# One layer of a gated three-branch decoder step: x loaded ahead of the modulation weights and kept transposed, the start ordered by hand, query statistics a step earlier

## The chip, the core and the metric

The kernel runs on one core of one Trainium2 chip. The time is the device time of one execution in microseconds (us); three runs of the kernel before have the median 1188.63. The engines are called PE (TensorE, the matrix multiplier), DVE (VectorE), ACT (ScalarE), POOL (GpSimd) and SP (SyncE, which here only issues DMAs). Each takes its instructions in the order in which they stand in its own queue.

## What is computed

Eight sample sequences of 8 tokens and one prompt of 1024 tokens, 1088 tokens of 1024 channels in all, pass one layer:

```python
mod = silu(c) @ ada_w + ada_b                      # c: one row for the prompt, eight for the samples
shift, scale, gate = split(mod, 3)
h = rmsnorm(x, norm_g) * (1.0 + scale) + shift
z = h @ w_in + b_in                                # some 8,500 + 3 * 1024 columns, split among:
ya = chunk_gmlp(a_u, a_v, ...) * silu(a_g)         # A: spatial gating in chunks of 128
yb = swa_branch(b_q, b_k, b_v, ...) * silu(b_g)    # B: sliding-window attention, 8 heads of 64, 2 of K and V
yc = mlstm_branch(c_qk, c_v, ...) * silu(c_g)      # C: matrix memory, short convolution on q and k
gates = sigmoid(m_g)                               # three per channel
merged = gates[0] * (ya @ w_branch_a) + gates[1] * (yb @ w_branch_b) + gates[2] * (yc @ w_branch_c)
x_out = x + gate * (merged @ w_out)
```

In branch B, q and k are normalised by head (an rmsnorm over 64 values) before the logits. The states of the branches are outputs as well.

## The kernel before

All is in float32. Matrix products are made of split operands: a high part, rounded to the multiplier's own format (float32r), and the rest, so that one product takes three matmuls (high by high, high by low, low by high). A split is a copy into the high part, mostly on ACT, and a subtraction on DVE. The names hh and hl are the high and low parts of h for each of its eight groups k of 128 channels, transposed to channels by tokens; hl without a number is also the name of a split slab of weights.

**The start** (the pool named start) makes h and the product with the first slab of w_in. x comes in nine tiles of 128 tokens (xt; the last, xts, holds the 64 sample tokens). A tile is squared and summed on ACT (L322), POOL makes the reciprocal root (L162 and L163) and DVE scales the tile in place (L325). The modulation comes in four blocks j, of two channel groups each: a block's weights are four loads of 512 KB (adaraw). PE multiplies them with silu(c) in 32 small matmuls (named adaraw,sT), ACT copies the result (msb, L356), PE turns it with eight matmuls (sel,msb), and DVE makes modA and modB of it (L366, L368). For a channel group k and a third ci of the tokens (384, 384 and 320 of them) three transposes on PE bring x into a PSUM tile (pk), ACT applies modA and modB (hf, L382), and DVE makes hh (L388) and hl (L389). Then PE multiplies with the two halves i of slab 0: 48 steps of three matmuls, 96 matmuls of 384 columns and 48 of 320. The weights of slab 0 are copied on ACT and subtracted on POOL (L277, L278).

The order of the start before is given by two strings. LOADS lists SP's loads: `x0 r x1 x2 a0 w0 a1 w1 x3 x4 x5 a2 x6 x7 x8 a3 s`, where a0 to a3 are the modulation's blocks, w0 and w1 the halves of slab 0, r and s small rows. STEPS is the order of the program, in which N is a group of three tiles of x, M a block, and 010 means groups 0 to 1 of third 0, each at once followed by its matmuls. A scheduler then orders each engine's instructions.

**Branch B** runs as a pipeline of 16 steps in two query groups g, eight token tiles n each, with other branches' products as filler; one step takes between 7 and 8 us. PE's order in it is that of the program. For each step the tile's queries are transposed on PE (L89), copied on ACT into the high part of QT (L1039) and subtracted on DVE (L1040). The statistics of the queries are made for three tiles at once (q_stats): squares and sums on DVE (L1011, L1012), a root on POOL. For the tiles 6 to 8 they are issued at step n = 6. Tile 8 holds the sample tokens: its queries are scaled ahead of the transposes, by two multiplications of 64x128 (qraw<-qraw,r, L1020), and split into QTs at step 7. K is transposed and split ahead of the pipeline into KT (L986, L987).

**The merge** has three rounds n of four pairs p. In a round PE makes the gates of a pair from h, and projects y with the branch weights (proj, which DVE evacuates at L1686); one pair takes some 33 us. Ahead of rounds 1 and 2, y_load reads the next branch's y from DRAM in eight pieces into a buffer of two halves (stage) and splits each piece into yh (ACT, L1649) and yl. The multiplication of branch B's result with its gate (gate_b) uses the same two halves for its two operands: it loads both, multiplies on DVE (L1757) and stores the product. Before, the multiplies of gate_b run as soon as their loads land.

Of the kernel before, what the change touches and what calls it, by code (L numbers as in the profile page):

```python
# [31 lines left out]
NORM1 = (0, 1, 2)  # L32
# [6 lines left out]
def trunk_kernel(ctx: ExitStack, tc: tile.TileContext, I, O):  # L39
# [197 lines left out]
    with tc.tile_pool(name="start", bufs=1, side="right", reuse_waits="tile") as st:  # L237
# [31 lines left out]

        hl0 = wp.tile([128, 2, 2112], F32R, tag="hl", bufs=2, name="hl")  # L270
        cur[0] = 1

        def slab0_load(i):
            raw = hp.tile([128, 1024], F32, tag=f"h{'hl'[i]}3", name="raw0")
            nc.sync.dma_start(raw.rearrange("p (k c) -> p k c", k=8), specs[0][i])
            o = slice(1024 * i, 1024 * i + 1024)
            S.copy(hl0[:, 0, o], raw)  # L277
            G.tensor_tensor(hl0[:, 1, o], raw, hl0[:, 0, o].bitcast(F32), ALU.subtract)  # L278
# [40 lines left out]
        def norm1(n):  # L319
            tn = TILES[n][1]  # L320
            junk = st.tile([128, 1024], F32, name="junk")
            S.activation(junk[:tn], xt[n][:tn], AF.Square, accum_out=ss[:tn, n:n + 1])  # L322
            y = rst[:, n:n + 1]
            rsqrt(y, ss[:, n:n + 1], 1024)
            V.tensor_scalar(xt[n][:tn], xt[n][:tn], y[:tn], None, ALU.mult)  # L325

        def norm(g):
            if g in NORM1:
                for n in range(3 * g, 3 * g + 3):
                    norm1(n)  # L330
                return
            sl = slice(3 * g, 3 * g + 3)
            for n in range(3 * g, 3 * g + 3):
                tn = TILES[n][1]
                junk = st.tile([128, 1024], F32, name="junk")
                S.activation(junk[:tn], xt[n][:tn], AF.Square, accum_out=ss[:tn, n:n + 1])
            rsqrt(rst[:, sl], ss[:, sl], 1024)
            for n in range(3 * g, 3 * g + 3):
                tn = TILES[n][1]
                V.tensor_scalar(xt[n][:tn], xt[n][:tn], rst[:tn, n:n + 1], None, ALU.mult)  # L340
# [7 lines left out]
        def mod(j):  # L348
# [7 lines left out]
            last["s"] = S.copy(msb, pm)  # L356
            pc = pk()
            if j == 0:
                tr(pc[:, 128:160], Ra)
                V.tensor_copy(cols[:, CADA:CADA + 32], pc[:, 128:160])  # L360
                V.tensor_scalar(cols[:, CADA + 8:CADA + 16], cols[:, CADA + 8:CADA + 16], 1.0, None, ALU.add)
            for q in range(4):
                mm(pc[:, 16 * q:16 * q + 9], msb[:, 128 * q:128 * q + 128], sel, True, True)
            for d in range(2):
                k = 2 * j + d
                last["m"] = V.tensor_scalar(modA[:, k], pc[:, 16 * d:16 * d + 9], cols[:, CADA + 8 + k:CADA + 9 + k],  # L366
                                cols[:, CNG + k:CNG + k + 1], ALU.add, ALU.mult)
                V.tensor_scalar(modB[:, k], pc[:, 32 + 16 * d:32 + 16 * d + 9], cols[:, CADA + k:CADA + k + 1],  # L368
                                None, ALU.add)

        def hprep(k, ci):
# [5 lines left out]
            px = pk()  # L377
            for i in range(3):
                t0, tn = TILES[3 * ci + i]
                tr(px[:, 128 * i:128 * i + tn], xt[3 * ci + i][:tn, 128 * k:128 * k + 128])  # L380
# [9 lines left out]
            if m < n:  # L390
                S.copy(hh[k][:, NT:1152], hlo[k][:, 1024:NT].bitcast(F32))
# [4 lines left out]
        def part(k, ci, i):  # L396
            c0, n = CH[ci]
            if (ci, i) not in acc:
                acc[ci, i] = pg() if 2 * ci + i < 3 else pu_()
# [8 lines left out]
        for step in STEPS.split():  # L408
            if step == "P":
                with tc.issue_after(last["m"].ins), tc.issue_after(last["s"].ins):  # L410
                    load_pieces(1, [None] * 3 + [st.tile([128, 528], F32, name="raw1")])
            elif step == "S":
                ps = pk()
                tr(ps[:, 0:68], R1)
                V.tensor_copy(cols[:, 0:CADA], ps[:, 0:CADA])
                V.tensor_copy(cols[:, CCB:100], ps[:, CADA:68])
            elif step[0] == "N":
                norm(int(step[1]))
            elif step[0] == "M":
                mod(int(step[1]))  # L420
            else:
                ci = int(step[2])
                for k in range(int(step[0]), int(step[1]) + 1):
                    hprep(k, ci)
                    for i in range(2 if ci < 2 else 1):
                        part(k, ci, i)
        for k in range(8):
            part(k, 2, 1)
# [419 lines left out]
    with tc.tile_pool(name="bph", bufs=1, side="right", reuse_waits="tile") as b1:  # L848
# [125 lines left out]
        def k_transpose(n):  # L974
# [9 lines left out]
            for g in range(2):  # L984
                o, i = slice(128 * n + 128, 128 * n + 256), slice(128 * g, 128 * g + 128)
                S.copy(KT[g][0][:, o], ps[:, i])  # L986
                V.tensor_tensor(KT[g][1][:, o], ps[:, i], KT[g][0][:, o].bitcast(F32), ALU.subtract)  # L987
# [18 lines left out]
        def q_stats(g, n0):  # L1006
# [7 lines left out]
            r3 = bt([128, 3, 4], "r3", bufs=2)  # L1014
            rsqrt(r3.rearrange("p n h -> p (n h)"), rf, 64)
            r3s[g] = r3
# [8 lines left out]
        def q_transpose(g, n):  # L1025
# [5 lines left out]
            for r in range(2):  # L1031
# [7 lines left out]
                S.copy(hi, src)  # L1039
                newq[0] = V.tensor_tensor(lo, src, hi.bitcast(F32), ALU.subtract).ins  # L1040
# [5 lines left out]
        class Prompt:  # L1046
# [224 lines left out]
        def a_norm():  # L1271
            vr = bt([128, 9], "vr", tag="rr", bufs=2)
            vq = bt([128, 9], "vq", tag="r3", bufs=2)
# [81 lines left out]
        for i in range(len(steps) + 6):  # L1355
            w = FILL[0] if i < 18 else FILL[1]
            for d, ph, share in PLAN:
                if 0 <= i - d < len(steps):
                    if ph == "q" and i < 16:
                        filler(0, ("q", i // 8, min(8, i % 8 // 3 * 3 + 2)))  # L1360
# [304 lines left out]
    def proj(n, f, Tt):  # L1665
# [5 lines left out]
        def run(t):  # L1671
            if n == 2 and f % 4 == 3:
                m_tiles(f)
            for h in range(2):
                for j in range(2):
# [9 lines left out]
                    with tc.high_priority():  # L1685
                        V.scalar_tensor_tensor(x, x, 1.0, ps, ALU.add, ALU.mult)  # L1686
# [9 lines left out]
    gst = {}  # L1696
# [53 lines left out]
    def gate_b(f, b):  # L1750
# [6 lines left out]
        V.tensor_tensor(x, x, y, ALU.mult)  # L1757
# [117 lines left out]
```

## Time and profile before

| | |
|---|---|
| median of three runs | 1188.63 us (1188.22 to 1191.99) |
| the profiled execution | 1185.67 us, span 1184.0 us |
| mean granted clock of PE | 0.997 |
| PE's waits over 1 us behind the first 60 us | 3.7, 1.2, 1.2 and 1.0 us |
| bytes moved | 129.73 MB, 110 GB/s over the span |

The profile is of one execution. A row of a timeline gives the start in us, the length, the engine, the line of the code, the instruction, what it writes and reads, the partitions by elements, and how many such stand in a row (x); in brackets how long the engine was idle before it, and what ended that. PE's instructions overlap, so that the time of one is read from the distance between two starts. A row of waits gives the engine, what it waited to do, the releaser, and us in total, times, and the longest. A row of windows gives the stretch, its length, the busy time of each engine, PE's granted clock (1.00 is full speed), the busy share of the DMA engines and the GB/s.

### The profile page before, as it was taken

The numbers are of one execution on the slowest core, as the hardware profiler recorded it, in microseconds if no ns is written. First come the engines' busy times: TensorE is split into PE (matmuls) and PEld (weight loads), VectorE is DVE, ScalarE is ACT, GpSimd is POOL, SyncE is SP. The second block draws the span as 40 slices with busy tenths as digits, with TensorE's granted clock in tenths as the row PEclk, the third lists the DMA queues.
The fourth block names the chain that finished last, engine by engine and source line by source line (L and its number), as shares of the span: only waits on it lengthen the run. The fifth ranks groups of instructions, "written<-read, shape, count | busy, mean of one in ns | idle before, by whom it ended". The sixth has DMA issues, their size and how long they took to land.

```text
span 1184.0 us, 23111 instructions
## 1 busy us (share of the span) xinstructions
PE 1154.9 (98%) x8924; PEld 1108.1 (94%) x8924; DVE 777.7 (66%) x1846; ACT 489.0 (41%) x1225; POOL 81.3 (7%) x111
## 2 busy tenths in 40 slices
PE   5899999999999999989999999999999999999998
PEld 2699999999999998978998999999999999999998
DVE  3577877655468587876598973655766676668433
ACT  4543455434343368877353441423322343235100
POOL 2100011102024001110000000000000000000000
PEclk9999999999999999989999999999999999999999
DMA  9821222323222110123235256424543354465422
GB/s 309 256 73 37 76 84 64 103 64 100 90 79 75 51 54 15 55 63 96 63 95 154 55 166 190 135 76 120 162 115 109 108 166 116 130 208 177 130 90 73
DMA packets 150773, 129.73 MB, mean 110 GB/s; under 512 B 13614, under 2 KB 140214, under 8 KB 150649
## 3 DMA queue, kind: packets, MB, share of 16 engines
q1 hardware_dynamic: 142984, 118.96, 34.1%
q0 software_dynamic: 2240, 7.08, 1.7%
q10 hardware_dynamic: 5440, 2.23, 0.7%
q8 instruction: 70, 1.15, 0.4%
q14 instruction: 39, 0.31, 0.1%
HBM read 99.39 MB, written 29.82 MB: 109 GB/s over the span
## 4 chain that ended last, share of the span: by engine, by line
PE 85%; DMA 5%; DVE 4%; ACT 2%; issue 1%; SPq 1%; POOL 0%; ACTq 0%; DVEq 0%
PE pg L85 47%; PE pk L85 22%; PE pu L85 13%; PE pk L89 2%; DMA stage<-dy 2%; DMA raw<-in_w_in_dram 1%; DMA dy<-stage 1%; SPq L251 1%; ACT Sm L1080 1%; DVE hl L125 1%; PE pu L89 1%; DVE Sm L1072 0%; DVE nm L1075 0%; DVE QT L1040 0%; DVE rr L1012 0%
## 5 line engine op out<-in xcount | busy, mean ns | idle before, releaser
L85 PE MATMUL pg<-hl,hl 128*128 128x256 f32 (+3 forms) x904 | 278.5, 308 | 0.8 <-DVE hl L389 0.8
L85 PE MATMUL pg<-hh,hl 128*128 128x384 f32 (+1 forms) x912 | 238.3, 335 | 3.4 <-DVE hh L388 2.3
L85 PE MATMUL pg<-hl,hh 128*128 128x256 f32 (+1 forms) x1008 | 178.0, 283 | 0.0
L85 PEld LDWEIGHTS pg<-hl,hl 128*128 128x128 f32 x904 | 170.9, 189 | 3.9 <-DVE hl L389 1.7
L85 PEld LDWEIGHTS pg<-hh,hl 128*128 128x128 f32 x912 | 161.9, 189 | 7.8 <-DVE hh L388 3.9
L85 PEld LDWEIGHTS pg<-hl,hh 128*128 128x128 f32 x1008 | 150.8, 189 | 0.3
L1408 ACT CAST prod<-raw 128x512 fp32r<-128x512 f32 x76 | 46.8, 620 | 125.0 <-PE pk L85 51.7
L85 PE MATMUL pg<-hh,prod 128*128 128x288 f32 (+1 forms) x400 | 83.9, 289 | 0.2 <-DVE prod L1409 0.2
L85 PE MATMUL pk<-hh,prod 128*128 128x256 f32 (+1 forms) x384 | 78.1, 285 | 0.0
L1572 ACT ACTIVATE tt<-tt,bh 128x288 f32<-128x288 f32 x96 | 49.8, 522 | 47.5 <-DVE tt L1517 16.2
L1409 DVE TENSOR_TENSOR prod<-raw,prod 128x512 fp32r<-128x512 f32 x76 | 51.8, 686 | 24.2 <-ACT prod L1408 24.0
L85 PEld LDWEIGHTS pg<-hh,prod 128*128 128x128 f32 x400 | 65.8, 188 | 1.1 <-issue 0.4
L85 PEld LDWEIGHTS pk<-hh,prod 128*128 128x128 f32 x384 | 62.6, 188 | 0.8 <-DVE tt L1526 0.4
L1408 ACT CAST prod<-comb 128x512 fp32r<-128x512 f32 x60 | 36.9, 615 | 62.1 <-PE pk L85 25.5
L85 PE MATMUL pg<-yh,prod 128*128 128x288 f32 (+1 forms) x288 | 60.9, 290 | 0.0
L85 PE MATMUL pk<-yh,prod 128*128 128x256 f32 (+1 forms) x288 | 58.7, 285 | 0.0
L85 PE MATMUL pg<-hl,prod 128*128 128x288 f32 (+1 forms) x200 | 57.7, 289 | 0.0
L85 PE MATMUL pu<-hh,prod 128*128 128x288 f32 (+1 forms) x272 | 56.3, 288 | 0.0
L85 PE MATMUL pk<-tc,prod 128*128 128x256 f32 (+1 forms) x408 | 56.2, 287 | 0.0
L85 PE MATMUL pg<-tc,prod 128*128 128x288 f32 (+1 forms) x396 | 55.7, 290 | 0.0
L85 PE MATMUL pk<-hl,prod 128*128 128x256 f32 (+1 forms) x192 | 54.6, 284 | 0.0
L85 PEld LDWEIGHTS pk<-tc,prod 128*128 128x128 f32 x408 | 52.6, 188 | 1.3 <-issue 0.8
(532 smaller groups left out, 2635.8 us busy)
## 6 DMA issues: line engine op xcount, KB each, us to landing
raw<-in_w_in_dram SPq DMA_DIRECT2D x124, 256.0 KB
adaraw<-in_ada_w_dram SPq DMA_DIRECT2D x16, 512.0 KB
stage<-dy SPq DMA_DIRECT2D x24, 272.0 KB
dmg<-tt SPq DMA_DIRECT2D x44, 144.0 KB
dmg<-tt SPq DMA_DIRECT2D x44, 128.0 KB
mprev<-dmg SPq DMA_DIRECT2D x32, 144.0 KB
xt<-in_x_prompt_dram SPq DMA_DIRECT2D x8, 512.0 KB
graw<-in_ada_w_dram SPq DMA_DIRECT2D x16, 256.0 KB
```

Of the source, the lines that this page charges most:

```text
L85: T.matmul(out, lhsT=lhsT, rhs=rhs, start=start, stop=stop)
L89: T.transpose(out, in_, ident[:k, :k])
L125: V.tensor_tensor(hl[:, 1, off:off + m], raw[:, :m], hl[:, 0, off:off + m].bitcast(F32), ALU.subtract)
L251: nc.sync.dma_start(raw.rearrange("p (k c) -> p k c", k=4), kv(ada_w[:, base:base + 256])[:, 4 * (q % 2):4 * (q % 2) + 4])
L1080: newS[0] = S.activation(Sm[:, h], Sm[:, h], AF.Exp, bias=nm[:, h:h + 1], scale=rr[:, h:h + 1], accum_out=dn[:, h:h + 1]).ins
L1408: a = S.copy(t[:, 0], x)
L1409: b = V.tensor_tensor(t[:, 1], x, t[:, 0].bitcast(F32), ALU.subtract)
L1572: S.activation(x, x, AF.Tanh, bias=bh[:, b:b + 1], scale=0.5)
```

## The change

Four things change.

**The start.** LOADS now brings all of x ahead of the blocks a1 to a3. STEPS becomes a list of single steps, and the four engines PE, ACT, DVE and POOL take their instructions in just this order (manual_schedule). A step is a letter and numbers: Q and N square and scale one tile of x, T transposes x for a channel group and a third, and copies it out of PSUM into a kept tile (xT, on ACT if k is 3 or 6, else on DVE), A and B are the two parts of a block's modulation, up to msb and from sel on, H makes hf, hh and hl, W splits half of slab 0 (the subtraction is now on DVE), G multiplies, P loads and splits slab 1, X writes paddings. The kept transposes of the groups 2 to 7 lie in the second buffer of the weight slabs and in free slots, and H reads them from there.

```diff
-LOADS = "x0 r x1 x2 a0 w0 a1 w1 x3 x4 x5 a2 x6 x7 x8 a3 s"
-STEPS = "N0 M0 010 M1 230 N1 M2 450 011 231 451 N2 M3 S 670 012 671 232 452 672 P"
+LOADS = "x0 r x1 x2 a0 x3 x4 x5 w0 x6 x7 x8 w1 a1 a2 a3 s"
+STEPS = """Q0 N0 Q1 N1 Q2 N2
+T20 T30 T40 A0 T50 T60 T70 Q3 B0 H00 H10 N3 Q4 N4 Q5 N5 W0
+H01 H11 T21 T31 G000 G100 T41 T51 G010 G110 T61 T71 Q6 N6 Q7 N7 W1 Q8 N8
+H02 H12 T22 G001 G101 T32 G011 G111 T42 T52 G020 T62 G120 T72 G021 G121
+A1 B1 H20 H30 H21 H31 G20 G30 H22 G21 H32 G31 A2 G22 B2 G32 H40 H50 H41 H51 G40 G50 H42 G41 H52 A3 G51
+B3 G42 H60 G52 H70 H61 H71 G60 H62 S G70 H72 P G61 G71 G62 G72 X"""
...
+        def slab0_split(i):
+            for j in range(2):
+                o, r = slice(1024 * i + 512 * j, 1024 * i + 512 * j + 512), raw0[i][:, 512 * j:512 * j + 512]
+                S.copy(hl0[:, 0, o], r)
+                V.tensor_tensor(hl0[:, 1, o], r, hl0[:, 0, o].bitcast(F32), ALU.subtract)
...
+        def x_keep(k, ci):
+            n = CH[ci][1]
+            px = x_transpose(k, ci)
+            kept_x[k, ci] = place(n)
+            if k % 3:
+                V.tensor_copy(kept_x[k, ci], px[:, :n])
+            else:
+                S.copy(kept_x[k, ci], px[:, :n])
...
+            px = kept_x[k, ci] if (k, ci) in kept_x else x_transpose(k, ci)
...
+        with tc.manual_schedule(engines={ET.PE, ET.Activation, ET.DVE, ET.Pool}):
+            for step in STEPS.split():
+                start_step(step)
```

ACT in the start, before, from the first block's msb on (junk,ss<-xt is a square of a tile, hl<-raw the copy of half of slab 0):

```order
L356 COPY msb<-pk 128x512
L277 CAST hl<-raw_130 128x1024
L382 ACTIVATE hf<-pk,modB,modA 128x384 x2
L277 CAST hl<-raw_142 128x1024
L356 COPY msb<-pk 128x512
L322 ACTIVATE junk,ss<-xt 128x1024 x2
```

ACT now, from behind the first block's msb on (xT<-pk is the copy of a kept transpose):

```order
L332 ACTIVATE junk,ss<-xt 128x1024
L407 ACTIVATE hf<-pk,modB,modA 128x384 x2
L332 ACTIVATE junk,ss<-xt 128x1024 x2
L287 CAST hl<-raw_137 128x512 x2
L407 ACTIVATE hf<-pk,modB,modA 128x384 x2
L397 COPY xT<-pk 128x384 x2
L332 ACTIVATE junk,ss<-xt 128x1024 x2
L287 CAST hl<-raw_145 128x512 x2
L332 ACTIVATE junk,ss<-xts 64x1024
```

Six squares now stand ahead of the second block's msb, and the last three of them behind two copies of transposes.

PE in the start, before, at the third block:

```order
L85 MATMUL pk<-adaraw,sT 32x256 x12
L85 MATMUL pk<-sel,msb 128x9 x4
L89 MATMUL pk<-ident,xt 128x128 x12
L85 MATMUL pg<-hh_387,hl 128x384 x2
L85 MATMUL pg<-hl_388,hl 128x384
```

PE now, at the second block:

```order
L89 MATMUL pk<-adaraw,sT 32x256 x16
L89 MATMUL pk<-sel,msb 128x9 x4
L89 MATMUL pg<-hh_506,hl 128x384
L89 MATMUL pg<-hl_507,hl 128x384
L89 MATMUL pg<-hh_506,hl 128x384 x2
```

The transposes that stood between a block's sel and its first matmul have moved ahead of the block.

**Query statistics.** For the tiles 6 to 8 they are made at step n = 5, and the splits of KT, QT and QTs are given priority in the scheduler.

```diff
-                if n % 3 == 0:
+                if n in (0, 3, 5):
                     with tc.issue_after(newq[0]):
-                        q_stats(g, n)
-                self.rr = r3s[g][:, n % 3]
+                        q_stats(g, (n + 1) // 3 * 3)
+                self.rr = r3s[g, n // 3][:, n % 3]
...
-                S.copy(hi, src)
-                newq[0] = V.tensor_tensor(lo, src, hi.bitcast(F32), ALU.subtract).ins
+                with tc.high_priority():
+                    S.copy(hi, src)
+                    newq[0] = V.tensor_tensor(lo, src, hi.bitcast(F32), ALU.subtract).ins
```

DVE at the end of the second query group, before (rr<-qs are the sums, qraw<-qraw,r the scaling of tile 8, QT<-pk,QT the low part of a tile's queries):

```order
L1012 TENSOR_REDUCE rr<-qs 128x3x2 x2
L1100 SCALAR_TENSOR_TENSOR Pp<-mcT,pu 128x512
L1085 TENSOR_TENSOR es<-es,dn 128x4
L1103 TENSOR_TENSOR Pc<-pu,mcT 128x512
L1072 COPY_PREDICATED Sm<-mprv,pk 128x256 x2
L203 TENSOR_TENSOR ts<-ts,pg 64x256
L1086 RECIPROCAL es<-es 128x4
L125 TENSOR_TENSOR hl<-raw,hl 128x512
L1040 TENSOR_TENSOR QT<-pk,QT 64x2x128
L1075 TENSOR_REDUCE nm<-Sm 128x4
L1228 TENSOR_TENSOR vn<-ts,avb 64x128 x2
L1020 TENSOR_TENSOR qraw<-qraw,r_6050 64x128 x2
```

DVE now, from the split of tile 6 on:

```order
L1067 TENSOR_TENSOR QT<-pk,QT 64x2x128
L1046 TENSOR_TENSOR qraw<-qraw,r_5959 64x128 x2
L207 TENSOR_TENSOR ts<-ts,pg 64x256
L129 TENSOR_TENSOR hl<-raw,hl 128x512
L1103 TENSOR_TENSOR nm<-nm,r_5714 128x4
L129 TENSOR_TENSOR hl<-raw,hl 128x512 x2
L1255 TENSOR_TENSOR vn<-ts,avb 64x128 x2
L1104 SCALAR_TENSOR_TENSOR nm<-nm,nsnk 128x4
L1255 TENSOR_TENSOR vn<-pg,avb 128x128
L840 TENSOR_TENSOR tc<-tx,tc 128x544
L1067 TENSOR_TENSOR QT<-pk,QT 64x2x128
```

The scaling stood between the two splits of tile 7 and stands now between those of tile 6.

**gate_b.** Its multiply is issued only behind the newest evacuation of a projection.

```diff
-                        V.scalar_tensor_tensor(x, x, 1.0, ps, ALU.add, ALU.mult)
+                        lastev[0] = V.scalar_tensor_tensor(x, x, 1.0, ps, ALU.add, ALU.mult).ins
...
-        V.tensor_tensor(x, x, y, ALU.mult)
+        with tc.issue_after(lastev[0]):
+            V.tensor_tensor(x, x, y, ALU.mult)
```

**y_load** for rounds 1 and 2 stands four items earlier in the list of the merge.

```diff
-                items.append((None, lambda _, n=n: y_load(n)))
+                items.insert(len(items) - 4, (None, lambda _, n=n: y_load(n)))
```

More of the change, by code (lines that the diff above doesn't have):

```diff
@@ L268, in x_load @@
             xt.append(xx)
+        xT0 = wp.tile([128, 2, 2112], F32, tag="hl", bufs=2, name="xT")
         hl0 = wp.tile([128, 2, 2112], F32R, tag="hl", bufs=2, name="hl")
         cur[0] = 1
+        raw0 = {}
         def slab0_load(i):
@@ L322, in norm1, with norm @@
             S.activation(junk[:tn], xt[n][:tn], AF.Square, accum_out=ss[:tn, n:n + 1])
[L323 to L340, printed above, removed]
+            rsqrt(rst[:, n:n + 1], ss[:, n:n + 1], 1024)
+        def norm(n):
+            tn = TILES[n][1]
+            V.tensor_scalar(xt[n][:tn], xt[n][:tn], rst[:tn, n:n + 1], None, ALU.mult)
         V.tensor_tensor(sel, ident[:, 0:9], ident[:, 32:41], ALU.add)
@@ L346, in trunk_kernel, with mod_a @@
         last = {}
-        def mod(j):
+        def mod_a(j):
             pm = pk()
@@ L355, in mod, with mod_b @@
             msb = st.tile([128, 512], F32, tag="msb", bufs=2, name="msb")
-            last["s"] = S.copy(msb, pm)
+            S.copy(msb, pm)
+            last["msb"] = msb
+        def mod_b(j):
+            msb = last["msb"]
             pc = pk()
@@ L406, in part, with start_step @@
                 conv_evac(xp0[i], 4 * i)(ci, c0, n, ps)
-        for step in STEPS.split():
+        def start_step(step):
+            d = [int(x) for x in step[1:]]
             if step == "P":
-                with tc.issue_after(last["m"].ins), tc.issue_after(last["s"].ins):
-                    load_pieces(1, [None] * 3 + [st.tile([128, 528], F32, name="raw1")])
+                load_pieces(1, [None] * 3 + [st.tile([128, 528], F32, name="raw1")])
             elif step == "S":
@@ L416, in trunk_kernel @@
                 V.tensor_copy(cols[:, CCB:100], ps[:, CADA:68])
[L417 to L420, printed above, removed]
-            else:
[L422 to L428, printed above, removed]
+            elif step[0] == "G":
+                for i in d[2:] or range(2):
+                    part(d[0], d[1], i)
+            else:
+                {"Q": squares, "N": norm, "W": slab0_split, "A": mod_a, "B": mod_b, "T": x_keep, "H": hprep, "X": pads}[step[0]](*d)
+        ET = mybir.EngineType
+        with tc.manual_schedule(engines={ET.PE, ET.Activation, ET.DVE, ET.Pool}):
+            for step in STEPS.split():
+                start_step(step)
         ps = pk()
@@ L1694, in proj @@
         items.append((prep, run))
-    gst = {}
+    gst, lastev = {}, [None]
     def gate_rows(g):
```

46 lines of the change are left out of this document (28 added, 18 removed).

## The prediction

> **What bounds the kernel now.** I read the page's busy times first, then the waits of TensorE (PE), then the table by windows, and last the timelines of the places that these name. Total busy time of PE, from the page:
>
> ```profile
> PE 1154.9 (98%) x8924; PEld 1108.1 (94%) x8924; DVE 777.7 (66%) x1846; ACT 489.0 (41%) x1225; POOL 81.3 (7%) x111
> ```
>
> So PE is the bound, and an edit pays only where PE stands still or runs slowly. PE's waits (us in total, times, longest), and three windows (length, then busy us of PE, its weight loads, DVE, ACT and POOL, granted clock, DMA share, GB/s):
>
> ```profile
> PE pk L89 <- ACT ts L1230: 3.7, 1, 3.7
> PE pk L89 <- DVE KT L987: 1.2, 1, 1.2
> PE pu L85 <- DVE tt L1518: 1.2, 1, 1.2
> PE pk L89 <- DVE qraw L1020: 1.0, 1, 1.0
> 20.00:40.00 20.00, 16.07 (x123) 9.77 (x124) 9.23 (x23) 10.21 (x18) 7.22 (x10) 1.00 1.08 343
> 60.00:80.00 20.00, 20.00 (x135) 18.52 (x136) 14.00 (x61) 11.83 (x28) 0.77 (x2) 1.00 0.20 55
> 500.00:520.00 20.00, 16.28 (x107) 15.11 (x107) 17.31 (x47) 16.95 (x61) 2.82 (x4) 0.89 0.24 67
> ```
>
> From about 60 us on PE fills whole windows. What can be won there are four single stalls, 7.1 us together. The 3.7 costs more than itself. PE's timeline around it, DVE's release of it, and the clock in 1 us windows:
>
> ```profile
> 508.74 0.51 PE L85 MATMUL pg<-hh,hl 128*128 128x384 f32 x2
> 509.09 0.34 PE L85 MATMUL pg<-hl,hl 128*128 128x384 f32 x1
> 511.96 0.38 PE L89 MATMUL pk<-ident,qraw 128*128 128x128 f32 x2
> 516.06 0.47 PE L89 MATMUL pk<-ident,qraw 64*128 64x64 f32 x2 [3.72 <-ACT ts L1230]
> 517.27 0.84 PE L85 MATMUL pg<-hh,hl 128*128 128x384 f32 x2
> 517.91 0.52 PE L85 MATMUL pg<-hl,hl 128*128 128x384 f32 x1
> 515.64 0.48 DVE L1020 TENSOR_TENSOR qraw<-qraw,r 64x128 f32<-64x128 f32 x2
> 516.00:517.00 1.00, 0.94 (x4) 0.85 (x5) 0.90 (x6) 0.52 (x4) 0.04 (x1) 0.50 0.00 0
> 522.00:523.00 1.00, 1.00 (x9) 0.59 (x6) 0.00 (x0) 0.60 (x2) 0.36 (x1) 0.88 0.00 0
> ```
>
> The PE row names ACT, but the transposed tile is qraw, which DVE scales at 515.64: that multiply ends the wait. After it two matmuls take 0.64 (517.27 to 517.91) where they took 0.35 (508.74 to 509.09): PE resumes at half clock and is at full clock again only in the window from 522, some 6.2 us later. So about 3.2 us more are lost, and the stall's price is 6.9.
>
> **The change, part by part.** *The 512 and 445 stalls.* The statistics of query tiles 6 to 8 are computed a step earlier, one step being some 7.6 us. In DVE's order, shown with the change, the scaling (qraw<-qraw,r) now stands between the two splits of tile 6 instead of those of tile 7, so it should be over some 4 us before PE asks. I take the whole price: -6.9 (bounds 0 and -7.2), and -1.0 for its twin at 445 (0 to -1.1). No DVE work is saved; it is spread over a step more.
>
> *Priority for the splits of KT.* DVE's rows around the 1.2 us wait for KT stand in the same order before and after: 0.
>
> *gate_b.* Its multiply now stands behind the projection's evacuation, so it no longer keeps DVE. DVE and PE there:
>
> ```profile
> 739.17 0.72 DVE L1757 TENSOR_TENSOR stage<-stage 128x544 f32<-128x544 f32 x1
> 740.77 0.37 PE L85 MATMUL pu<-yh,prod 128*128 128x288 f32 x1 [1.16 <-DVE tt L1518]
> 817.83 1.20 ACT L1649 CAST yh<-stage 128x544 fp32r<-128x544 f32 x2 [4.26 <-PE pu L85]
> 833.73 0.65 ACT L1649 CAST yh<-stage 128x544 fp32r<-128x544 f32 x1 [2.15 <-DMA stage<-dy]
> 839.63 0.29 PE L85 MATMUL pk<-yh,prod 128*128 128x288 f32 x1
> ```
>
> -1.2. The price: the stage buffers stay with gate_b until the first round of projections ends at about 818, where two of the eight loads of the next y used to lie in them (the first two casts at 817.83 wait for no DMA). The other six took until 833.73, some 2.6 each; two more put the last cast at 839 to 841, where PE wants it from 839.63 on. I take +1 (0 to 4).
>
> *The start.* The same matmuls, and 18 copies of transposed x more: 12 on DVE, 6 on ACT. The trace has no such copy; its bounds are 0.35 (the nearest smaller copy out of PSUM, convst, by the view of groups) and the 0.67 that ACT takes to read as much in hf, of which I take 0.6. The subtraction of slab 0 moves from POOL to DVE, beside transposes, at no cost. What counts is the order. In ACT's order, shown with the change, the last three squares (of x6, x7 and xts) wait behind copies of transposes that PE makes late, and PE's next work waits for these squares. Rows that price this:
>
> ```profile
> 9.50 1.06 ACT L322 ACTIVATE junk<-xt 128x1024 f32<-128x1024 f32 x1 [0.58 <-DMA xt<-in_x_prompt_dram]
> 10.46 0.19 ACT L322 ACTIVATION_READ_ACCUMULATOR junk<-xt 128x1 f32 x1
> 11.59 0.75 DVE L325 TENSOR_SCALAR xt<-xt,rstd 128x1024 f32<-128x1024 f32 x1 [0.96 <-POOL rstd L163]
> 12.32 0.90 PE L89 MATMUL pk<-ident,xt 128*128 128x128 f32 x3
> 13.15 1.94 PE L85 MATMUL pk<-adaraw,sT 128*32 128x256 f32 x16
> 26.52 1.06 ACT L322 ACTIVATE junk<-xt 128x1024 f32<-128x1024 f32 x1
> 27.71 1.06 ACT L322 ACTIVATE junk<-xt 128x1024 f32<-128x1024 f32 x1
> 28.77 1.22 ACT L382 ACTIVATE hf<-pk,modB,modA 128x384 f32<-128x384 f32 x2
> 34.52 1.50 PE L85 MATMUL pk<-adaraw,sT 128*32 128x256 f32 x24
> 36.73 1.06 PE L85 MATMUL pk<-sel,msb 128*128 128x9 f32 x8 [0.70 <-ACT msb L356]
> 37.64 1.98 PE L89 MATMUL pk<-ident,xt 128*128 128x128 f32 x12
> 39.89 0.62 PE L85 MATMUL pg<-hh,hl 128*128 128x384 f32 x2 [0.27 <-DVE hh L388]
> 55.49 0.77 PE L89 MATMUL pk<-ident,xt 128*128 128x128 f32 x5 [0.40 <-DVE modB L368]
> 66.97 0.41 PE L85 MATMUL pg<-hl,hh 128*128 128x264 f32 x2
> 67.22 0.38 PE L89 MATMUL pk<-ident,xt 128*128 128x128 f32 x2
> 70.20 0.31 PE L85 MATMUL pu<-hl,hl 128*128 128x320 f32 x1
> 70.35 0.45 PE L85 MATMUL pu<-hh,hl 128*128 128x320 f32 x2
> 75.18 0.31 PE L85 MATMUL pu<-hh,hl 128*128 128x320 f32 x1
> ```
>
> (a) PE begins at 12.34, when the third tile is scaled: nine transposes (0.83 for three) to 14.8, 32 rows of A0 to about 18, msb, sel to about 20.2, first modulation at 20.7, two hf to 21.9. (b) ACT squares x4 and x5 to 24.3; from a square's end (10.65) to the scaled tile (12.34) are 1.7 us: 26.0. From 21 to 26 PE has some transposes and stands. (c) Then 19 transposes (0.14 each) and 12 matmuls (0.175) to the transpose that ACT waits for: 4.8 at full clock. As after 512.3, where clock and idle together lasted 10 us, half clock holds until about 31: 33.2. (d) Copy 0.6, two squares 2.4, two casts 1.2, a square 1.25, scaling 1.5: 40.2. PE stands nearly 7 us. (e) Left then are 96 adaraw rows (6.0), 24 sel (2.7), some 24 transposes (4), 84 matmuls of 384 (14.6) and 48 of 320 at 0.15 (7.1): 34.4. (f) After each of the three modulations PE waits for mod, hf and hh, as PE's order now has nothing between sel and the first matmul, where twelve transposes stood. The whole way is 0.7 ahead of sel and 2.25 behind it (37.64 to 39.89); later blocks hide most of it in matmuls, so 4.5 for all three. (g) Half clock after the 7 us: 2.5 (2 to 3.2). End: 40.2 + 34.4 + 4.5 + 2.5 = 81.6. Before, the last matmul of this part ends at about 75.3, with eight of the next slab's in between (0.125 each): 74.3. The start costs +7.3 (+1.5 to +9.5).
>
> [...]
>
> **Sum.** -6.9 - 1.0 + 0 - 1.2 + 1 + 7.3 = -0.8. The profiled execution took 1185.67, with a span of 1184.0, and would take 1184.9; the runs' median is 3 higher, 1188.63, and becomes 1187.8. About 0.3% (3.6 us) is what a measurement of this kernel can tell from no change.
>
> **Rivals.** *The clock holds (0.20).* The idle stretches of the start are broken by single transposes, and stalls of up to 1.2 us left the clock at full. Then (c) is 2.4 shorter and (g) is nothing: 4.9 less than the forecast, 1182.9, faster. [...]
>
> *The start runs ahead (0.05).* If the order of ACT doesn't hold PE, the loads of x do. Behind the third tile (landed at 9.50) are 5.5 MB up to the last, at 343 GB/s over at 25.5: squared and scaled at 28.4, plus 34.4 and 4.5 gives 67.3, 14.3 less than the forecast: 1173.5. Against it stands ACT's order above.
>
> *The scaling is still late (0.14), slower.* DVE is busy for 17.31 us of the window from 500, more than PE (16.28); if the earlier statistics push its queue so that the scaling or a QT split still comes over 3 us after 512.3, the 6.9 stay and the start's loss is bare: 1194.7.
>
> *y late (0.08).* At 4 us instead of 1: 1190.8.
>
> **How the numbers follow.** The forecast, with single terms off by 2 or 3, has 0.50; 0.03 is for the rest. Faster: 0.08 of the forecast, most of the first rival, all of the second: 0.31. Slower: most of the third, and parts of the fourth and the forecast: 0.20. Same: 0.49. The range 1180 to 1195 holds all but the second rival and the ends of the first and third; the forecast alone spans 1184 to 1192.
>
> **What would show it.** In the profile after: PE's waits without the rows at 445 and 512, clock 1.00 there; between 20 and 41 us two idle stretches, of 4 to 5 and of 6 to 7 us, ended by scaled x, and a granted clock of 0.5 behind the second; the last matmul of the start near 81; DVE's stage multiply without a DMA wait. I am wrong if the start ends before 77, or if PE waits for qraw near 510.

## The result, and the profile after

The changed kernel took 1199.52 us (median of five runs, 1196.54 to 1201.82) against 1188.63 before: a ratio of 1.0083, with an interval of [1.0057, 1.0108]. Five later runs of it, beside other kernels of the study, had 1201.03 and a ratio of 1.0101 [1.0081, 1.0120]. The forecast was 1187.8, about no change; what came is a loss of some 0.9%.

The profiled execution took 1201.82, with a span of 1200.1, so it is 16.1 longer than the one profiled before. PE's busy time and its longer waits, from the page and the view of waits (us in total, times, longest):

```profile
PE 1161.1 (97%) x8924; PEld 1115.8 (93%) x8924; DVE 789.1 (66%) x1862; ACT 490.2 (41%) x1233; POOL 76.2 (6%) x109
```

```profile
PE pk L93 <- DVE xt L337: 14.1, 8, 3.1
PE pk L93 <- DVE th L317: 5.9, 1, 5.9
PE pg L89 <- DVE hh L413: 2.7, 2, 1.6
PE pk L89 <- ACT yh L1676: 2.3, 1, 2.3
PE pg L89 <- ACT prod L1435: 2.1, 1, 2.1
PE pk L93 <- DVE xts L337: 1.9, 1, 1.9
PE pk L93 <- DVE KT L1013: 1.2, 1, 1.2
PE pk L93 <- DVE Sm L1099: 0.7, 1, 0.7
```

The 5.9 for th lies ahead of PE's first matmul, and was 5.7 before. The 3.7 for ts, the 1.0 for qraw and the 1.2 for tt are gone, and the 1.2 for KT stands as before. New are two waits that the sum didn't have in this size or at all: 2.3 for yh, the next branch's y, and 2.1 for prod, the first weights of the merge. Both cost twice in this execution, by the windows (same columns as in the prediction; 840 to 860 holds the wait for yh, 600 to 610 that for prod):

```profile
20.00:40.00 20.00, 9.13 (x48) 7.56 (x47) 13.21 (x28) 11.00 (x20) 6.05 (x11) 0.76 1.10 328
40.00:60.00 20.00, 17.49 (x95) 13.31 (x96) 9.57 (x28) 6.06 (x11) 0.00 (x0) 0.76 0.59 187
60.00:80.00 20.00, 18.66 (x150) 15.42 (x150) 11.51 (x37) 7.35 (x13) 0.00 (x0) 0.97 0.00 1
500.00:520.00 20.00, 20.00 (x168) 18.43 (x168) 17.19 (x49) 14.26 (x57) 4.70 (x3) 1.00 0.05 14
840.00:860.00 20.00, 17.52 (x116) 16.96 (x116) 14.43 (x29) 8.76 (x17) 0.00 (x0) 0.83 0.57 167
...
520.00:530.00 10.00, 9.25 (x62) 7.71 (x59) 9.63 (x30) 9.90 (x37) 2.00 (x2) 1.00 0.44 120
600.00:610.00 10.00, 8.07 (x50) 7.84 (x51) 6.81 (x12) 4.97 (x10) 0.54 (x1) 0.83 1.03 302
```

The stretch from 500 is now full and at full clock. The matmuls that stood at 512 come at 525 here, and there too the clock is full; only the 0.7 for Sm is left. The start is at 0.76 for 40 us, and behind each of the two new waits the clock falls.

As both kernels run the same 8924 matmuls, their starts can be laid beside each other, and the difference read as it grows. In time of the kernel before, it is +12.6 at 96 us, behind the start; +1.0 up to 147; -1.0 at 447 and +0.5 at 451; -5.6 at 512 (3.0 of the wait and 2.6 of half clock); +3.7 at 592 (the wait for prod 2.1, half clock 1.6); -1.4 at 741; +5.8 from 841 on (the wait for yh 2.5, half clock 3.3). That is 15.6 of the 16.1.

This pair of executions overstates the loss. The profiled execution of the kernel before is among its fastest (1185.67 against 1188.63), the one of the kernel after the slowest of its five. Where these 3 us may lie is found below.

### The profile page after: what moved, and what is told of

It is laid out like the page before. It is cut to its first block, busy times and chain, and to the rows that moved or that the text cites. A ratio compares the mean times of both kernels' runs of the same rounds, so it can differ in the third digit from the quotient of the medians.

```text
span 1200.1 us, 23137 instructions
## 1 busy us (share of the span) xinstructions
PE 1161.1 (97%) x8924; PEld 1115.8 (93%) x8924; DVE 789.1 (66%) x1862; ACT 490.2 (41%) x1233; POOL 76.2 (6%) x109
## 4 chain that ended last, share of the span: by engine, by line
PE 85%; DVE 7%; DMA 3%; ACT 2%; issue 1%; POOL 0%; SPq 0%; DVEq 0%; ACTq 0%; POOLq 0%
PE pg L89 45%; PE pk L89 24%; PE pu L89 13%; PE pk L93 2%; DMA stage<-dy 1%; DVE hl L129 1%; DVE acc L494 1%; PE pu L93 1%; DMA raw<-in_w_in_dram 1%; DMA xt<-in_x_prompt_dram 0%; DVE vv L535 0%; DMA Cs<-in_state_mlstm_C_dram 0%; ACT junk L332 0%; DMA E<-scr 0%; DMA dy<-stage 0%
```

## The experiments

Each of them was timed in five rounds against the kernel before on the same chip, whose median was 1187.6 to 1188.4 throughout; after a ratio stands its interval.

| kernel | median, us | ratio to before |
|---|---|---|
| the changed kernel, again | 1201.03 | 1.0101 [1.0081, 1.0120] |
| changed, with the start of before | 1186.50 | 0.9981 [0.9966, 0.9996] |
| changed, gate_b and y_load of before | 1196.94 | 1.0057 [1.0039, 1.0076] |
| changed, gate_b alone of before | 1195.83 | 1.0054 [1.0039, 1.0070] |
| changed, squares ahead of H01 | 1192.59 | 1.0031 [1.0019, 1.0043] |
| changed, raw tiles of the merge first | 1198.41 | 1.0082 [1.0066, 1.0099] |
| changed, step S and H72 earlier | 1200.38 | 1.0096 [1.0078, 1.0114] |
| changed, sel of 120 columns | 1199.38 | 1.0092 [1.0070, 1.0115] |
| before, other slab buffer | 1190.41 | 1.0029 [1.0012, 1.0045] |
| before, the earlier statistics and the priority of the splits | 1183.34 | 0.9943 [0.9923, 0.9962] |
| before, sel of 120 columns | 1191.00 | 1.0017 [1.0004, 1.0031] |
| changed, squares and A1 earlier, gate_b and y_load of before | 1186.03 | 0.9979 [0.9968, 0.9990] |
| another list of steps and loads, gate_b and y_load of before, raw tiles first | 1175.92 | 0.9893 [0.9874, 0.9912] |
| the same, sel of 120 columns | 1174.69 | 0.9885 [0.9861, 0.9908] |

**The start alone undone.** The changed kernel with LOADS, STEPS and the functions of the start as before.

> The changed kernel with the start of the kernel before (its loads, its steps, the scheduler's order); the query statistics, gate_b and y_load stay changed. My theory: the start costs about 13 us, not the 7 forecast, and it also moves the weight slabs to the other of their two buffers, which costs 2 to 3 us more where the merge begins. So this takes 1184 to 1187, PE's last matmul of the start ends near 75, and the wait for the first weights of the merge (2.1 us near 601) is gone. Rival 1: the start costs the 7 us of the forecast and the rest was lost elsewhere: about 1192. Rival 2: the start is not what costs: 1199.

It took 1186.5, so the whole of the loss, and more, lies on the start and on what the start does to the slabs' memory. By ratios (1.0083 over 0.9981) that is some 12 us, and 14 by the 1.0101 of the later runs.

**The other slab buffer.** The wait for prod is no part of the start, yet it went with the start. SP's queue in the changed kernel, where the first raw weights of the merge are asked for, and the matmul that waits for them (start, length; the row of SP spans seven loads):

```profile
597.99 6.16 SPq L1425 DMA_DIRECT2D raw<-in_w_in_dram  x7
```

```profile
601.73 0.40 PE L89 MATMUL pg<-hh,prod 128*128 128x288 f32 x1 [2.08 <-ACT prod L1435]
```

and in the kernel before:

```profile
556.82 37.54 SPq L1398 DMA_DIRECT2D raw<-in_w_in_dram  x7
```

The first load leaves 41 us later, in a kernel that is some 8 us behind at that place. xT, the kept x, takes the first of the two buffers for slabs, so every later slab lies in the other buffer than before, and the last slab now lies where the merge puts its first raw tile. That tile can't be loaded until the last matmul has read the slab, at about 598. To show this without the rest of the change, the kernel before got a tile in front, of which a single column is written and nothing read:

```diff
+        spare = wp.tile([128, 2, 2112], F32, tag="hl", bufs=2, name="spare")
+        V.memset(spare[:, 0, 0:1], 0.0)
```

> The kernel before with one thing more: a tile that nobody reads, of the size of a split weight slab, is taken ahead of slab 0, so that every slab lies in the other of the two buffers. No work is added but one small memset on DVE. My theory: the first weight load of the merge then lies over the last slab and waits for the end of its matmuls, as in the changed kernel, so PE waits about 2 us near 592, and at times runs at half clock behind it: +2 to +3.5, 1190.5 to 1192. Rival: the wait in the changed kernel comes from the later start or from the statistics: no change, 1188.6.

It is 2.8 slower than the kernel before, with the same late load (597.45) and a wait of 1.9 for prod: an idle tile costs what xT costs. The cure from the other side, in the changed kernel, is to let the pool of the raw tiles (w2) take its memory ahead of the two pools that stood before it:

```diff
+    w2 = ctx.enter_context(tc.tile_pool(name="w2", bufs=1, reuse_waits="tile"))
     e2 = ctx.enter_context(tc.tile_pool(name="e2", bufs=1, reuse_waits="tile"))
     w3 = ctx.enter_context(tc.tile_pool(name="w3", bufs=1, reuse_waits="tile"))
-    w2 = ctx.enter_context(tc.tile_pool(name="w2", bufs=1, reuse_waits="tile"))
```

> The changed kernel in which the pool of the merge's raw tiles takes its memory ahead of the two others, so that none of the first raw loads lies in the buffer of the last slab. If the wait of 2.1 us at 602 comes from that overlap alone, it is gone, with the half clock behind it where that fell: 2 to 3.3 us less than the changed kernel, and the first raw load is issued some 40 us earlier. Rival: the splits of these weights are late for another reason (their order on ACT and DVE): no gain.

SP's row for the same loads:

```profile
565.57 37.54 SPq L1425 DMA_DIRECT2D raw<-in_w_in_dram  x7
```

The load leaves early again, the wait for prod is gone from the list of waits, and the median is 2.6 below that of the changed kernel beside it (1201.03). The intervals of the two overlap, and against the first runs (1199.52) the gain is only 1.1. The wait for yh, further on, is 2.9 here and 2.4 in the profile of the kernel beside it, so that a part of what was won is lost again there.

**Which edit makes y late.** First both edits of the merge undone, then gate_b's wait alone:

```diff
-        with tc.issue_after(lastev[0]):
-            V.tensor_tensor(x, x, y, ALU.mult)
+        V.tensor_tensor(x, x, y, ALU.mult)
```

> The changed kernel with gate_b and y_load as before. My theory: the multiply of gate_b behind the last evacuation keeps the two stage halves until PE is through the first round, so y's eight loads come late; undone, PE's 2.3 us of waits for y near 852 and the half clock behind it (3 us) go, and the 1.2 us wait near 751 comes back: -4 to -5, 1194.5 to 1195.5. Rival: y is late because all before it is late, or because the loads share bandwidth: no change, 1199.5.

> The changed kernel in which the multiplies of gate_b run as soon as their loads land, as before, while y_load keeps its new place in the list of items. If it is gate_b's wait that holds the stage buffers and makes y late, this kernel loses the 2.3 us wait for yh near 850 and the half clock behind it, as the one with both edits undone did: about 3 less than the changed kernel, some 1194 to 1195. Rival: it is the new place of y_load that makes y late; then this kernel is like the changed one, 1197 to 1199.

The two are alike (1.0057 and 1.0054), and both lie 3 to 5.5 below the changed kernel (1.0083 and 1.0101). So it is gate_b's wait, and beside it the place of y_load does nothing that these runs can tell. DVE's idle time ahead of gate_b's multiplies did fall as intended, from 17.1 to 1.9. The chain in the changed kernel, on SP (the last store of gate_b, the first load of y), on ACT (the last split of y) and on PE:

```profile
830.50 0.32 SPq L1786 DMA_DIRECT2D dy<-stage  x1
830.87 0.42 SPq L1675 DMA_DIRECT2D stage<-dy  x1
```

```profile
852.61 0.65 ACT L1676 CAST yh<-stage 128x544 fp32r<-128x544 f32 x1 [0.54 <-DMA stage<-dy]
```

```profile
853.30 0.61 PE L89 MATMUL pk<-yh,prod 128*128 128x288 f32 x1 [2.33 <-ACT yh L1676]
```

The loads of y begin only behind the last store, and the eighth piece is split 22 us later. PE resumes at half clock, by the window of its first us:

```profile
853.00:854.00 1.00, 0.61 (x1) 0.29 (x1) 0.71 (x2) 1.00 (x3) 0.00 (x0) 0.50 0.21 78
```

In the kernel whose gate_b is free, ACT's first and last split of y:

```profile
827.67 1.20 ACT L1676 CAST yh<-stage 128x544 fp32r<-128x544 f32 x2 [4.26 <-PE pu L89]
...
843.43 0.65 ACT L1676 CAST yh<-stage 128x544 fp32r<-128x544 f32 x1 [2.05 <-DMA stage<-dy]
```

Two pieces are in the stage buffers before the projections let go of yh, and the last split is 9 us earlier. PE no longer waits for yh in this profile.

**The statistics alone.** The kernel before with only the query statistics a step earlier, and the priority of the splits that belongs to them.

> The kernel before with only the query statistics a step earlier, and nothing else of the change (start, gate_b and y_load as before). By the offsets of the two profiles the stall at 512 gave back 3.0 us of idle time and 2.4 of half clock, and its twin at 445 1.0: 6.4 less than the kernel before, about 1181. The prediction's term was 7.9, about 1180. Rival, from the medians of the first runs: the kernel with the start of before gained 1.1 and lost some 3 by gate_b and y_load, so the statistics are worth only 4: about 1183.5.

0.9943 is 6.8 less, 4.5 to 9.1 by the interval: the term of 7.9 holds. At the same place a wait of 0.8 for Sm is left, which was hidden in the 3.7.

**The squares ahead of H01.** The changed kernel, with the last three squares out of their place behind the copies of transposes:

```diff
-H01 H11 T21 T31 G000 G100 T41 T51 G010 G110 T61 T71 Q6 N6 Q7 N7 W1 Q8 N8
+Q6 N6 Q7 N7 Q8 N8 H01 H11 T21 T31 G000 G100 T41 T51 G010 G110 T61 T71 W1
```

> The changed kernel with one edit in the order of the start: squares and scaling of the last three tiles of x (Q6 N6 Q7 N7 Q8 N8) stand ahead of H01 instead of behind T71; loads, copies and work stay. My theory: the last squares waited on ACT behind copies of late transposes, and PE for them; without that the long idle stretch from 34 to 40 shrinks and the half clock behind it goes: the start ends near 79 instead of 87, -6 to -8, about 1192.5. Rival 1: the copies of x and the late loads of the modulation weights are what costs: within 1 us of 1199.5. Rival 2: the squares then delay hf of H01 and the idle time only moves ahead: -2 to 0.

1192.59: by the ratios 6 to 8 below the changed kernel, and in the profiles a matmul behind the start (the 561st) comes 6.1 earlier. The second idle stretch, which stood at 33 to 40, is gone. The first is not: it now ends at 28.8, and its first wait is again 3.09, as the squares of x4 and x5 still stand behind the first two hf.

**The second modulation spread too.** The two parts A1 and B1 moved in among transposes and matmuls, the squares as above, gate_b and y_load as before.

> The changed kernel with gate_b and y_load as before, the squares and scalings of the last three tiles ahead of H01, and the second modulation's two parts A1 and B1 ahead of and behind H02 and H12, so that transposes and matmuls stand between them and the first matmul that needs them. If the start is lost to the order of steps, and the waits behind the modulation and the third stretch at half clock with them, it ends about 9 us earlier than in the changed kernel (the squares alone took 6 to 7): some 1187 to 1188, 9 below the kernel that only has gate_b as before. Rival: the waits behind the second modulation move to another place: the gain is that of the squares alone, about 1190.

1186.03, and the same matmul 9.2 earlier than in the changed kernel: another 3.1 for the spread modulation, by single profiles, and 3 to 5 are left for gate_b.

**All steps spread.** x is loaded ahead of a1 to a3 as in the change, and x6 also ahead of slab 0, whose halves change places. The list takes the squares and scalings of the tiles 3 to 8 among the first transposes and matmuls, and each modulation in two parts with other work between. Its first third:

```diff
-LOADS = "x0 r x1 x2 a0 x3 x4 x5 w0 x6 x7 x8 w1 a1 a2 a3 s"
+LOADS = "x0 r x1 x2 a0 x3 x4 x5 x6 w1 w0 x7 x8 a1 a2 a3 s"
+STEPS = """Q0 N0 Q1 N1 Q2 N2 T10 T30 A0 Q3 T60 T40 Q4 T50 B0 N3 Q5 T70 N4 Q6 N5 H00
+W1 H01 W0 T41 G001 H10 N6 G000 T21 Q7 T61 T20 Q8 G011 G101 N8 N7 G010 T31 H11 A1 T51 T22 B1
...
```

> The changed kernel with another list of single steps: the squares of the tiles 4 to 8 early, the modulations one by one spread among matmuls, the loads of x6 ahead of slab 0, the second modulation's weights as before behind all of x; gate_b and y_load as before; the memory of the merge's raw tiles allocated first, so that they don't lie in the last slab's buffer. If x early and transposed early is no cost in itself, and the loss is all in the order of the steps, a walk through the queues with the trace's durations ends the start at 66 us instead of 86; with 3 for gate_b and 3 for the merge that is 1171 to 1173. Rival: the loads (the last of x at some 26 us, the weights of the second modulation behind it) hold the start near the 74 to 77 of the kernel before: 1179 to 1182.

1175.92, 1.1% below the kernel before. PE's idle time where the first stretch was, in this kernel:

```profile
22.46 0.33 PE L88 MATMUL pk<-ident,xt 128*128 128x128 f32 x1 [0.80 <-DVE xt L332]
23.59 0.33 PE L88 MATMUL pk<-ident,xt 128*128 128x128 f32 x1 [0.80 <-DVE xt L332]
24.78 1.11 PE L88 MATMUL pk<-ident,xt 128*128 128x128 f32 x4 [0.86 <-DVE xt L332]
```

and in the changed kernel:

```profile
24.09 0.47 PE L93 MATMUL pk<-ident,xt 128*128 128x128 f32 x1 [3.09 <-DVE xt L337]
25.28 0.48 PE L93 MATMUL pk<-ident,xt 128*128 128x128 f32 x1 [0.72 <-DVE xt L337]
26.74 2.40 PE L93 MATMUL pk<-ident,xt 128*128 128x128 f32 x10 [0.99 <-DVE xt L337]
...
36.22 0.30 PE L93 MATMUL pk<-ident,xt 128*128 128x128 f32 x1 [3.08 <-DVE xt L337]
37.60 0.48 PE L93 MATMUL pk<-ident,xt 128*128 128x128 f32 x1 [1.08 <-DVE xt L337]
39.98 0.36 PE L93 MATMUL pk<-ident,xts 64*128 64x64 f32 x1 [1.91 <-DVE xts L337]
...
54.16 1.06 PE L89 MATMUL pk<-sel,msb 128*128 128x9 f32 x8 [0.70 <-ACT msb L353]
56.87 0.44 PE L89 MATMUL pg<-hh,hl 128*128 128x384 f32 x1 [1.65 <-DVE hh L413]
69.04 0.44 PE L89 MATMUL pg<-hh,hl 128*128 128x384 f32 x1 [1.04 <-DVE hh L413]
85.50 0.42 PE L89 MATMUL pu<-hh,hl 128*128 128x320 f32 x1 [0.66 <-DVE ff L558]
```

The wait for x5 ends 2 us earlier and the stretch before x8 is gone. The 561st matmul comes 13.7 earlier, where the walk of the expectation had 20: the clock is halved once more from 38 to 45 (below), and a load of the second modulation's weights holds PE for 1.1. So x loaded early and kept transposed need cost nothing; the order of the steps decides. No run takes the new list with the loads of the changed kernel, so that the share of the three moved loads in this is not shown.

**The tail of the start.** ACT waits 3.23 there for the column constants, one of its two longest waits late in the start:

```profile
83.54 1.06 ACT L230 ACTIVATE xpad<-pg,cols 128x384 f32<-128x384 f32 x2 [3.23 <-DVE cols L443]
84.49 0.59 ACT L407 ACTIVATE hf<-xT,modB,modA 128x256 f32<-128x256 f32 x1
```

```diff
-B3 G42 H60 G52 H70 H61 H71 G60 H62 S G70 H72 P G61 G71 G62 G72 X
+B3 S G42 H60 G52 H70 H61 H71 G60 H62 H72 G70 P G61 G71 G62 G72 X
```

> The changed kernel with step S (the column constants) ahead of H60 instead of behind H62, and H72 ahead of G70. If the end of the start loses time because ACT's evacuations wait for constants that stand behind H62 on DVE, and the last hf waits behind these evacuations, the start ends 1.5 to 2.5 us earlier. Rival: PE is full there with matmuls that need neither, and the wait on ACT costs nothing: no gain.

My theory falls. The wait is gone from ACT (the first xpad runs at 82.28), and the time is the same: 1200.38 beside 1201.03. PE had other matmuls meanwhile, and waited for 0.66 in the changed kernel.

**What the clock counts.** In the changed kernel the clock is halved from 57.63 to 61.04, behind a window in which PE ran the eight small matmuls of a modulation and stood twice. Padding sel from 9 to 120 columns leaves their number alone:

```diff
-                mm(pc[:, 16 * q:16 * q + 9], msb[:, 128 * q:128 * q + 128], sel, True, True)
+                mm(pc[:, 120 * q:120 * q + 120], msb[:, 128 * q:128 * q + 128], selw, True, True)
```

> The changed kernel in which the matrix sel, that turns the modulation's row into columns, is padded with zeros from 9 to 120 columns, in the start alone: the same number of matmuls. Each took 0.11 between two starts with 9 columns, where a transpose of 128 columns took 0.115. If matmuls of 9 columns count as idle for the clock, the window from 54.2 to 57.6, with these eight matmuls and two idle stretches, no longer halves the clock: no half clock near 58 to 61, 1.7 us less, 1197 to 1199 beside 1199 to 1201 for the changed kernel. Rival: the clock goes by the time in which any matmul runs: the half clock there stays, and the time.

> The kernel before with the same padding of sel. In four profiles of its start the clock was halved in 0, 2, 2 and 3 stretches, three of them behind a window with eight of these matmuls, and the start ended up to 7 us apart. If these matmuls count as idle, the padding takes away two of the stretches in most executions: 2 to 4 us less than the kernel before, some 1185. Rival: the time in which any matmul runs decides: no change, 1188.

> The kernel with all steps ahead (x early, spread modulations, gate_b and y_load as before), with the same padding of sel. Its profile had half clock from 38.0 to 44.9, behind a window with seven of these matmuls that was about half busy. If they count as idle, this stretch goes: up to 3.4 less, 1172.5 to 1174. Rival: no change, 1176.

The windows on both sides of the drop, of the changed kernel and then of the one with wide matmuls:

```profile
54.22:57.63 3.41, 1.61 (x10) 1.26 (x11) 1.98 (x8) 1.91 (x4) 0.00 (x0) 1.00 0.41 164
57.63:61.04 3.41, 3.41 (x12) 3.41 (x13) 3.13 (x10) 1.58 (x3) 0.00 (x0) 0.50 0.00 0
```

```profile
53.29:56.70 3.41, 1.57 (x9) 1.16 (x9) 1.89 (x7) 1.71 (x4) 0.00 (x0) 1.00 0.45 173
56.70:60.12 3.42, 3.27 (x11) 3.25 (x11) 3.18 (x10) 1.92 (x4) 0.00 (x0) 0.50 0.04 18
```

The drop stays, with PE busy for as much of the window before it (1.57 us, and 1.61 with narrow matmuls). So it wasn't the narrowness of these matmuls that let the clock fall; that the time in which PE stands decides fits this, but isn't shown. The changed kernel is the same, the kernel before 0.2% slower (its scheduler moved some steps of the start as well). The fastest kernel is 1.2 lower, with overlapping intervals; its second half clock is gone in the profile (1.00 from 40 to 60 us, where it was 0.88), but one execution can't tell whether the padding did that or where the windows fell.

## Why the prediction was wrong, point by point

The sum was -0.8, and by the ratios of the runs it is about +10 to +12. The experiments allow each part a size of its own, by runs where there are such:

- *The 512 and 445 stalls, -7.9.* Right: -6.8 alone. In the profiles 6.1, as half clock had cost less (2.6, not 3.2), a wait of 0.7 for Sm comes next, and one of 0.5 for QT came in at 451.
- *KT, 0.* Right: 1.2 before, 1.2 after.
- *gate_b, -1.2, and y_load, +1 (0 to 4).* Their sum, -0.2, is where a step failed. The mechanism was named rightly: the stage buffers stay with gate_b and the y loads that used to be early come late. I put the last split at 839 to 841 in time of the kernel before; it came at 852.61, which with the 10 us of shift at that place is 842.6. A delay of 2.3 then fell on a full PE and halved the clock, 3.3 more. The gain at 741 was 1.4. In runs the pair costs 3 to 5.5. The price of a wait with the clock behind it stood two paragraphs above, in the 512 stall, and I didn't apply it here. It isn't paid each time: in the changed kernel with the start of before a wait of 2.4 for yh had no half clock behind it (shown in the last section).
- *The start, +7.3.* Right in sign and mechanism. Steps (a) to (d) came out within 0.8: hf to 22.1, the first stretch to 26.74 (26.0), the copy that the squares wait for at 32.85 (33.2), PE resuming at 39.98 (40.2). The waits behind the modulations, (f), are 0.70, 1.65 and 0.15, then 1.04, then 0.15; with 0.66 for another operand (ff) near the end they make 4.35 (4.5). That total agrees in part by luck, as the last modulation cost almost nothing. Step (g) failed: its 2.5 for half clock was an estimate that no run shows, and 10.8 us at half clock, from 39.98 to 47.39 and from 57.63 to 61.04, cost 5.4 if all of it ran at half speed. The clock, at 0.50 from 37.15 to 47.39, came back only 7.4 us after PE had resumed, and it fell a third time, in the waits of (f) (0.50 from 57.63 to 61.04). The other 2.7 up to the end at 86.9 are in gaps too short to be listed and in work that I had rounded down.
- *The slabs' memory, not in the sum.* +2.6 to +2.8. That xT lies in a buffer of the slabs stands in the change; what that does to every later slab, and to what is laid over the last one, was not followed.
- *The base.* The end of the start before, 74.3, was a lucky one. Three other profiles with that start have the 561st matmul at 99.1, 100.7 and 103.3 us, where the profiled one has 95.9. It had no half clock in its start (1.00 in each 20 us up to 100), they have two, two and three stretches (down to 0.84, 0.83 and 0.83). This can account for the 3 us by which the profiled execution undercuts its median. It also makes the start's loss smaller than the 12.6 of the pair of profiles: the four profiles with the old start have this matmul at 99.7 in the mean, and five with the changed start, from 108.5 to 109.9, at 109.1, which is 9.4 later (a rough figure, as the four spread over 7 us).

So the parts in runs are about -6.8, +4.5, +9.5 and +2.7: +9.9. The 4.5 is what the runs with the start of before leave beside the statistics, and the 9.5 is the rest of the whole, so this sum had to come out; what bears it out are the 3 to 5.5 of the runs with gate_b free and the 9.4 of the profiles. With the 1201.03 of the later runs the rest would be 2 more. Of the 10.7 by which the sum was off, y has 4.7, the slabs 2.7, the start 2.2 and the statistics 1.1.

Of the rivals, *the clock holds* is refuted (0.76 for 40 us), *the scaling is still late* too. *y late* was the one that came true, with the clock on top. *The start runs ahead*, at 67.3, did not come here; it is what a better order of steps approaches: the fastest kernel's start ends near 69.5. Neither of the two signs of being wrong that the prediction named came up: one looked for a start that ends early, the other for the wait near 510, and none for a start that ends late or for waits in the merge.

## What to carry to other kernels

Price each delay on a full PE as the wait and a half clock that may follow it: where it did, 2.1 to 3.7 us of waiting cost 1.6 to 3.3 more here. When a buffer of a rotating pair goes to something new, follow which half every later tenant gets, up to the first tile that is laid over the pair when its pool closes. And when an order is written by hand, ask of each engine what stands behind an instruction that waits: three squares and scalings moved ahead of other work were worth 6 to 8 us.

## What was not expected of the hardware

In the profiles before and after, the clock changed only from one window of 3.41 us to another. In the changed kernel half clock lasted 6.83 us from 23.50 and from 852.93, 10.24 from 37.15, and 3.41 from 57.63 and from 603.76; in the kernel before it lasted 6.83 from 515.42. These are one to three times 3.41, and full clock lasts whole windows too: the 245.76 us from 607.17 to 852.93 are 72. Counted from the first instruction, an edge of these windows lies at 0.01 in the profile before and at 3.02 in the one after, so where they fall on the work is not the same. None of the six windows ahead of a drop was without work: PE was busy for 0.30 to 1.83 us of each. In the prediction's own stall, 512.01 to 515.42, it was 0.33. The window from 54.22 to 57.63, with PE busy for 1.61 of 3.41 us by the profile, was followed by half clock, and so was this one of the kernel with all steps spread, with 2.36:

```profile
34.63:38.04 3.41, 2.36 (x25) 1.57 (x21) 2.37 (x4) 0.59 (x1) 0.00 (x0) 1.00 1.10 347
38.04:44.87 6.83, 6.83 (x39) 4.20 (x42) 3.77 (x12) 2.29 (x4) 0.00 (x0) 0.50 1.07 339
```

Other windows in which PE was busy for less than these 2.36 us stayed at full clock and were followed by it (2.22 from 67.87 to 71.28 in the changed kernel, 2.20 from 375.47 to 378.89 in the kernel before), so that these runs give no threshold.

Whether a wait is followed by half clock was open from one execution to the next. The waits of 2.1 for prod and 2.3 for yh in the changed kernel's profile were (0.50 from 603.76 and from 852.93). Three others behind the start were not: of 2.4 for yh in the changed kernel with the start of before, of 2.0 for prod in the one with squares and A1 earlier, and of 2.2 for prod in the one with gate_b alone of before. The mean clocks of these three profiles, 0.994, 0.994 and 0.991, are worth some 14, 14 and 21.5 us of half clock, and the first 80 us alone hold 13.6, 13.6 and 20.4 of it (in steps of 20 us 0.99, 0.84, 0.93 and 0.90; 1.00, 0.74, 0.98 and 0.94; 1.00, 0.77, 0.76 and 0.96), so that no stretch of 3.41 is left for the wait. Half clock came with the waits of 3.7 in the kernel before (0.50 from 515.42 to 522.25) and in the same kernel with sel of 120 columns (0.66 from 520 to 530), and behind the start with none of the waits of up to 1.2 in the profiles before and after. In the same way the start of before had none to three such stretches (0, 2, 2 and 3 in four profiles), and ended some 7 us apart at most (its 561st matmul at 95.9 to 103.3): a single profile of a start with gaps is one draw of several.
